# RMSNorm with GELU on one core: row squares and 1/rms moved to VectorE, one whole last store, gamma in two transfers

## The chip, the cores and the metric

The kernel runs on one core of a Trainium2 chip; the other cores run nothing. Profiles name the engines of a core so: PE is TensorE (PEld its weight loads), DVE is VectorE, ACT is ScalarE, POOL is GpSimd, SP is SyncE; 16 DMA engines move data between HBM and the core's memory. The metric is the device time of one execution in microseconds, as a median of several executions. A profiled execution gives a span, from its first to its last instruction, about 2 us under the time. Every execution told of here is at a granted clock of 1.0.

## The reference

```python
batch, seq_len, hidden = 8, 1024, 2048          # x: 64 MiB of float32
rms = np.sqrt(np.mean(x ** 2, axis=-1, keepdims=True) + eps)
out = gamma * x / rms
return 0.5 * out * (1 + np.tanh(np.sqrt(2 / np.pi) * (out + 0.044715 * out ** 3)))
```

The 8192 rows are independent. The output is as large as the input, so 67.1 MB come in and 67.1 MB go out.

## The kernel before

The rows are taken in 16 groups of 128 partitions x 4 rows x 2048 columns, 4 MiB each, which rotate through six buffers. A group is loaded from the queue of SP; ACT squares each row and sums it; POOL makes 1/rms of the sums; DVE multiplies by gamma (spread over the partitions once, in PSUM); ACT applies GELU with 1/rms as its scale and stores from its own queue. A buffer is loaded again when its store has landed.

```python
store_pieces = {
    0: [(R, [(0, NARROW), (NARROW, R * D)])],              # a narrow first piece
    G - 1: [(1, [(r * D, r * D + D)]) for r in range(R)],   # last group: a store for each row
}
scale_pieces = {G - 1: [(0, 1), (1, 1), (2, 1), (3, 1)]}

def squares(g):                                             # ACT
    for r in range(R):
        nc.scalar.activation(out=junk, in_=slot[g % SLOTS][:, r, :],
                             func=ACT.Square, accum_out=ssq[:, g, r : r + 1])

def inverse_rms(g):                                         # POOL, six small operations
    v = nc.gpsimd
    v.tensor_scalar(out=ms, in0=ssq[:, g, :], ...)          # mean + eps
    v.tensor_tensor(out=y, in0=ms, in1=power, op=ALU.pow)   # ** -0.5
    ...                                                     # one Newton step, four operations

# ... cut: scale (DVE), gelu_store (ACT)
for k in range(0, D, CHUNK):                                # CHUNK = 512: four transfers
    nc.scalar.dma_start(out=gamma_row[...], in_=gamma[k : k + CHUNK]...)
for g in range(SLOTS):
    load(g)
# ... cut
for g in range(G + 1):
    if g < G:
        squares(g); inverse_rms(g); scale(g)
    if g:
        gelu_store(g - 1)
        if g - 1 + SLOTS < G:
            load(g - 1 + SLOTS)
```

Of the kernel before, what the change touches and what calls it, by code (L numbers as in the profile page):

```python
# [1 line left out]

# [4 lines left out]

FP32 = mybir.dt.float32
ALU = mybir.AluOpType
ACT = mybir.ActivationFunctionType  # L10

P = 128
ROWS = 4
SLOTS = 6

GW = 32
CHUNK = 512

NARROW = 128


@with_exitstack
def kernel(
    ctx: ExitStack,
    tc: tile.TileContext,
    x: bass.AP,
    gamma: bass.AP,
    eps: bass.AP,
    out: bass.AP,
):  # L30




    nc = tc.nc
    D = x.shape[-1]
    R = ROWS
    eps_f = float(eps)
    x3 = x.rearrange("b s d -> (b s) d").rearrange("(g p r) d -> g p r d", p=P, r=R)
    o3 = out.rearrange("b s d -> (b s) d").rearrange("(g p r) d -> g p r d", p=P, r=R)  # L40
    G = x3.shape[0]

    sbuf = ctx.enter_context(tc.tile_pool(name="sbuf", bufs=1))
    psum = ctx.enter_context(
        tc.tile_pool(name="psum", bufs=1, space=bass.MemoryType.PSUM)
    )
    slot = [sbuf.tile([P, R, D], FP32, name=f"slot{i}") for i in range(SLOTS)]
    gamma_row = sbuf.tile([1, D // GW, GW + 4], FP32, name="gamma_row")
    ones = sbuf.tile([1, P], FP32, name="ones")
    warm = sbuf.tile([1, 1], FP32, name="warm")  # L50
    power = sbuf.tile([P, R], FP32, name="power")
    ssq = sbuf.tile([P, G, R], FP32, name="ssq")
    rstd = sbuf.tile([P, G, R], FP32, name="rstd")
    ms = sbuf.tile([P, R], FP32, name="ms")
    y = sbuf.tile([P, R], FP32, name="y")
    z = sbuf.tile([P, R], FP32, name="z")
    gamma_ps = psum.tile([P, D], FP32, name="gamma_ps")
    junk = psum.tile([P, D], FP32, name="junk")


    whole = [(R, [(0, R * D)])]
    store_pieces = {
        0: [(R, [(0, NARROW), (NARROW, R * D)])],
        G - 1: [(1, [(r * D, r * D + D)]) for r in range(R)],
    }
    scale_pieces = {G - 1: [(0, 1), (1, 1), (2, 1), (3, 1)]}

    def load(g):
        nc.sync.dma_start(out=slot[g % SLOTS], in_=x3[g])  # L69

    def squares(g):
        for r in range(R):
            nc.scalar.activation(  # L73
                out=junk,
                in_=slot[g % SLOTS][:, r, :],
                func=ACT.Square,
                accum_out=ssq[:, g, r : r + 1],
            )

    def scale(g):  # L80
        for r, n in scale_pieces.get(g, [(0, R)]):
            rows = slot[g % SLOTS][:, r : r + n, :]
            nc.vector.tensor_tensor(  # L83
                out=rows,
                in0=rows,
                in1=gamma_ps.unsqueeze(1).to_broadcast([P, n, D]),
                op=ALU.mult,
            )

    def inverse_rms(g):  # L90

        v = nc.gpsimd
        v.tensor_scalar(  # L93
            out=ms, in0=ssq[:, g, :], scalar1=1.0 / D, scalar2=eps_f,
            op0=ALU.mult, op1=ALU.add,
        )
        v.tensor_tensor(out=y, in0=ms, in1=power, op=ALU.pow)  # L97
        v.tensor_tensor(out=z, in0=y, in1=y, op=ALU.mult)  # L98
        v.tensor_tensor(out=z, in0=z, in1=ms, op=ALU.mult)  # L99
        v.tensor_scalar(  # L100
            out=z, in0=z, scalar1=-0.5, scalar2=1.5, op0=ALU.mult, op1=ALU.add
        )
        v.tensor_tensor(out=rstd[:, g, :], in0=z, in1=y, op=ALU.mult)  # L103

    def gelu_store(g):
        flat = slot[g % SLOTS].rearrange("p r d -> p (r d)")
        dst = o3[g].rearrange("p r d -> p (r d)")
        row = 0
        for n, stores in store_pieces.get(g, whole):
            for r in range(row, row + n):  # L110
                nc.scalar.activation(  # L111
                    out=slot[g % SLOTS][:, r, :],
                    in_=slot[g % SLOTS][:, r, :],
                    func=ACT.Gelu_apprx_tanh,
                    scale=rstd[:, g, r : r + 1],
                )
            row += n
            for a, b in stores:
                nc.scalar.dma_start(out=dst[:, a:b], in_=flat[:, a:b])  # L119

    with tc.manual_schedule():
        for k in range(0, D, CHUNK):
            nc.scalar.dma_start(
                out=gamma_row[:, k // GW : (k + CHUNK) // GW, 0:GW],
                in_=gamma[k : k + CHUNK].rearrange("(o a b) -> o a b", o=1, b=GW),
            )
        for g in range(SLOTS):
            load(g)
        nc.gpsimd.memset(power, -0.5)  # L129
        nc.vector.memset(warm, 0.0)  # L130
        nc.vector.memset(ones, 1.0)  # L131
        nc.scalar.activation(out=warm, in_=warm, func=ACT.Gelu_apprx_tanh)  # L132
        for k in range(0, D, CHUNK):
            nc.tensor.matmul(  # L134
                out=gamma_ps[:, k : k + CHUNK],
                lhsT=ones,
                rhs=gamma_row[:, k // GW : (k + CHUNK) // GW, 0:GW],
                start=True,
                stop=True,
            )  # L140
        for g in range(G + 1):
            if g < G:
                squares(g)
                inverse_rms(g)
                scale(g)
            if g:
                gelu_store(g - 1)
                if g - 1 + SLOTS < G:
                    load(g - 1 + SLOTS)


# [1 line left out]
_INS = ['x', 'gamma', 'eps']  # L153
_OUTS = [((8, 1024, 2048), 'float32')]

_NUMBERS = {'eps': 9.999999747378752e-06}


# [26 lines left out]
```

## Time and profile before

| | before |
|---|---|
| time, three runs | 317.45 us (317.38 to 317.48) |
| ACT / DVE / POOL busy | 251.2 / 139.4 / 32.3 us of 315.5 |
| DMA: 134.25 MB over the span | 426 GB/s |
| one square on ACT, with the read of its sum | 1.881 + 0.186 us |
| one multiplication by gamma, four rows | 8.69 us |

### The profile page before, as it was taken

What the parts mean: (1) busy time and instruction counts of PE and PEld (TensorE: products, weight loads), DVE (VectorE), ACT (ScalarE), POOL (GpSimd) and SP (SyncE); (2) the same over time, 40 slices, a digit from 0 to 9 for tenths busy, and PEclk for the clock granted to TensorE, in tenths of its full rate; (3) what the DMA queues carried; (4) which work ended last, traced back from release to release, by engine and by line L of the source; (5) the groups of instructions that cost most, each with busy time, mean ns of one, the idle gap of its engine ahead of it and who ended that gap; (6) DMA issues with size and microseconds to landing.
All of it is one profiled execution on the core that took longest, in us unless ns stands there. A gap on an engine that the chain in (4) does not pass through costs nothing.

```text
span 315.5 us, 479 instructions
## 1 busy us (share of the span) xinstructions
PE 7.9 (3%) x8; PEld 2.1 (1%) x8; DVE 139.4 (44%) x21; ACT 251.2 (80%) x194; POOL 32.3 (10%) x101
## 2 busy tenths in 40 slices
PE   0810000000000000000000000000000000000000
PEld 0200000000000000000000000000000000000000
DVE  0028909091918282827328082370824609480000
ACT  1289999999999999989596895969959599598500
POOL 0020202020202020202020020200202002020000
DMA  8999999999999999999999999999999999999997
GB/s 329 404 461 403 459 413 396 453 406 462 403 461 407 457 407 458 411 453 416 449 428 440 432 432 432 432 440 424 446 416 453 411 453 411 453 415 449 416 418 314
DMA packets 5315, 134.25 MB, mean 426 GB/s; under 512 B 704, under 2 KB 832, under 8 KB 832
## 3 DMA queue, kind: packets, MB, share of 16 engines
q1 hardware_dynamic: 2304, 67.11, 49.7%
q10 hardware_dynamic: 3008, 67.12, 49.4%
q14 instruction: 3, 0.02, 0.0%
HBM read 67.12 MB, written 67.11 MB: 425 GB/s over the span
## 4 chain that ended last, share of the span: by engine, by line
ACT 38%; DMA 32%; another core or an unknown queue 18%; issue 5%; ACTq 1%; SPq 0%
ACT slot L111 21%; DMA slot<-in_x_dram 16%; ACT junk L73 16%; DMA out_dram<-slot 15%; ACTq L119 1%; SPq L69 0%; ACTq L111 0%; ACTq L73 0%
## 5 line engine op out<-in xcount | busy, mean ns | idle before, releaser
L83 DVE TENSOR_TENSOR slot<-slot,gamma_ps 128x8192 f32<-128x8192 f32 (+1 forms) x19 | 139.2, 7338 | 142.3 <-ACT junk L73 142.3
L73 ACT ACTIVATE junk<-slot 128x2048 f32<-128x2048 f32 x64 | 120.4, 1881 | 40.8 <-DMA slot<-in_x_dram 36.8
L111 ACT ACTIVATE slot<-slot,rstd 128x2048 f32<-128x2048 f32 x64 | 123.0, 1987 | 1.7 <-ACT slot L111 1.7
L93 POOL TENSOR_SCALAR ms<-ssq 128x4 f32<-128x4 f32 x16 | 3.1, 194 | 242.8 <-ACT junk L73 242.8
L97 POOL TENSOR_TENSOR y<-ms,power 128x4 f32<-128x4 f32 x16 | 16.1, 1009 | 1.3
L73 ACT ACTIVATION_READ_ACCUMULATOR junk<-slot 128x1 f32 x64 | 11.9, 186 | 0.0
L134 PE MATMUL gamma_ps<-gamma_row,ones 1*128 1x512 f32 x8 | 7.9, 1112 | 9.2 <-DMA gamma_row<-in_gamma_dram 9.2
L132 ACT ACT_TABLE_LOAD x1 | 1.3, 1283 | 3.3 <-issue 3.3
L99 POOL TENSOR_TENSOR z<-z,ms 128x4 f32<-128x4 f32 x16 | 3.2, 201 | 1.3
L103 POOL TENSOR_TENSOR rstd<-z,y 128x4 f32<-128x4 f32 x16 | 3.2, 200 | 1.3
L98 POOL TENSOR_TENSOR z<-y 128x4 f32<-128x4 f32 x16 | 3.2, 200 | 1.3
L100 POOL TENSOR_SCALAR z<-z 128x4 f32<-128x4 f32 x16 | 3.1, 195 | 1.4
L134 PEld LDWEIGHTS gamma_ps<-gamma_row,ones 1*128 1x128 f32 x8 | 2.1, 306 | 13.4 <-issue 8.7
L130 DVE MEMSET warm<- 1x1 f32 x1 | 0.1, 59 | 0.8 <-PEq L166 0.8
L132 ACT ACTIVATE warm<-warm 1x1 f32<-1x1 f32 x1 | 0.2, 203 | 0.0
L131 DVE MEMSET ones<- 1x128 f32 x1 | 0.2, 165 | 0.0
L129 POOL MEMSET power<- 128x4 f32 x1 | 0.1, 102 | 0.3 <-POOLq L166 0.3
L166 POOL MEMSET const-float32-0.0<- 128x1 f32 x1 | 0.1, 99 | 0.2 <-issue 0.2
L166 POOL MEMSET const-bfloat16-1.0<- 128x1 bf16 x1 | 0.1, 102 | 0.0
L166 POOL MEMSET const-uint8-127<- 128x1 uint8 x1 | 0.1, 102 | 0.0
L166 POOL MEMSET const-float32-1.0<- 128x1 f32 x1 | 0.1, 99 | 0.0
## 6 DMA issues: line engine op xcount, KB each, us to landing
slot<-in_x_dram SPq DMA_DIRECT2D x16, 4096.0 KB, 29.9
out_dram<-slot ACTq DMA_DIRECT2D x14, 4096.0 KB, 43.3
out_dram<-slot ACTq DMA_DIRECT2D x4, 1024.0 KB, 17.5
out_dram<-slot ACTq DMA_DIRECT2D x1, 4032.0 KB, 28.5
gamma_row<-in_gamma_dram ACTq DMA_DIRECT2D x4, 2.0 KB, 10.3
out_dram<-slot ACTq DMA_DIRECT2D x1, 64.0 KB, 14.4
```

The lines of the kernel that those rows point to most:

```text
L73: nc.scalar.activation(out=junk, in_=slot[g % SLOTS][:, r, :], func=ACT.Square, accum_out=ssq[:, g, r : r + 1],)
L83: nc.vector.tensor_tensor(out=rows, in0=rows, in1=gamma_ps.unsqueeze(1).to_broadcast([P, n, D]), op=ALU.mult,)
L93: v.tensor_scalar(out=ms, in0=ssq[:, g, :], scalar1=1.0 / D, scalar2=eps_f, op0=ALU.mult, op1=ALU.add,)
L97: v.tensor_tensor(out=y, in0=ms, in1=power, op=ALU.pow)
L98: v.tensor_tensor(out=z, in0=y, in1=y, op=ALU.mult)
L99: v.tensor_tensor(out=z, in0=z, in1=ms, op=ALU.mult)
L100: v.tensor_scalar(out=z, in0=z, scalar1=-0.5, scalar2=1.5, op0=ALU.mult, op1=ALU.add)
L103: v.tensor_tensor(out=rstd[:, g, :], in0=z, in1=y, op=ALU.mult)
L111: nc.scalar.activation(out=slot[g % SLOTS][:, r, :], in_=slot[g % SLOTS][:, r, :], func=ACT.Gelu_apprx_tanh, scale=rstd[:, g, r : r + 1],)
L119: nc.scalar.dma_start(out=dst[:, a:b], in_=flat[:, a:b])
L132: nc.scalar.activation(out=warm, in_=warm, func=ACT.Gelu_apprx_tanh)
L134: nc.tensor.matmul(out=gamma_ps[:, k : k + CHUNK], lhsT=ones, rhs=gamma_row[:, k // GW : (k + CHUNK) // GW, 0:GW], start=True, stop=True,)
```

## The change

The intent is to relieve ACT, to shorten the small chain that makes 1/rms, and to have fewer transfers. In each group one or two of the four row squares go to DVE (22 of 64). All of 1/rms but the power goes to DVE, in four operations in place of five. The last group has one store in place of four. Gamma comes in two transfers in place of four; its row is now the first partition of the buffer that takes the throw-away squares of DVE.

```diff
-GW = 32
-CHUNK = 512
+GW = 64
+CHUNK = 1024
-    gamma_row = sbuf.tile([1, D // GW, GW + 4], FP32, name="gamma_row")
+    spare = sbuf.tile([P, D // GW, GW + 8], FP32, name="spare")
+    gamma_row = spare[0:1]
-        G - 1: [(1, [(r * D, r * D + D)]) for r in range(R)],
+    flat_pieces = {0: [(0, NARROW), (NARROW, R * D)]}
+    def on_vector(g):
+        return 1 if g % 3 else 2
+    def squares_on_vector(g, r, n):
+        for q in range(r, r + n):
+            row = slot[g % SLOTS][:, q, :].rearrange("p (a b) -> p a b", b=GW)
+            nc.vector.scalar_tensor_tensor(
+                out=spare[:, :, 0:GW], in0=row, scalar=1.0, in1=row,
+                op0=ALU.bypass, op1=ALU.mult, accum_out=ssq[:, g, q : q + 1])
-        v = nc.gpsimd
+        v = nc.vector        # ... the power alone stays on nc.gpsimd, then three operations
-                squares(g)
-                inverse_rms(g)
-                scale(g)
+                squares(g, 0, R - on_vector(g))
+                squares_on_vector(g, R - on_vector(g), on_vector(g))
+                # ... inverse_rms and scale; in the last group scale of row 0 comes first
```

## The prediction

> **What bounds the kernel now.** I read the engine shares first, then the transfer rates, then the waits, and only then the two ends of the span in order of time. From the page of the profiled run of the kernel before:
>
> ```profile
> span 315.5 us, 479 instructions
> ...
> PE 7.9 (3%) x8; PEld 2.1 (1%) x8; DVE 139.4 (44%) x21; ACT 251.2 (80%) x194; POOL 32.3 (10%) x101
> ...
> DMA  8999999999999999999999999999999999999997
> GB/s 329 404 461 403 459 413 396 453 406 462 403 461 407 457 407 458 411 453 416 449 428 440 432 432 432 432 440 424 446 416 453 411 453 411 453 415 449 416 418 314
> ...
> q1 hardware_dynamic: 2304, 67.11, 49.7%
> q10 hardware_dynamic: 3008, 67.12, 49.4%
> ```
>
> No compute engine is full: ACT has 80%, and it is what the change relieves. The DMA row has a 9 in every slice but the first and the last, and the two queues together took 49.7 + 49.4 = 99.1% of the 16 engines' span. 0.991 x 315.5 = 312.6 us of packet time on each engine, in a span of 315.5. So 2.9 us at most are not packet time, and those are the first microseconds before a packet moves and the last ones after it. The bytes are the same after the change: 16 loads and 16 stores of 4 MiB.
>
> The same over stretches (columns: stretch, length, busy time of PE, PEld, DVE, ACT, POOL, clock, DMA share, GB/s):
>
> ```profile
> 60.00:270.00 210.00, 0.00 (x0) 0.00 (x0) 104.25 (x12) 182.24 (x140) 23.98 (x72) 1.00 1.00 434
> 270.00:300.00 30.00, 0.00 (x0) 0.00 (x0) 8.88 (x4) 23.58 (x16) 2.00 (x6) 1.00 1.00 431
> 304.00:313.00 9.00, 0.00 (x0) 0.00 (x0) 0.00 (x0) 0.00 (x0) 0.00 (x0) 1.00 1.01 425
> 314.00:315.50 1.50, 0.00 (x0) 0.00 (x0) 0.00 (x0) 0.00 (x0) 0.00 (x0) 1.00 0.00 0
> ```
>
> DMA share is 1.00 from 60 to 313 us, with compute beside it or without. From 304 to 313 us no engine does anything, and the stores alone fill the DMA engines. The rate there is 425 GB/s, not 434: that is the last group, cut in four. The waits say who is early:
>
> ```profile
> POOL ms L93 <- ACT junk L73: 242.8, 16, 20.8
> DVE slot L83 <- ACT junk L73: 142.3, 16, 20.6
> ACT junk L73 <- DMA slot<-in_x_dram: 36.8, 10, 8.7
> ```
>
> DVE and POOL wait for ACT, and ACT waits for loads. A quicker ACT therefore only waits longer for loads. The chain of waits itself names ACT with 38%, but it is a chain through whichever wait came last, and the rows above show that for all of its length the DMA engines were full. I give the chain no weight.
>
> The tail, in order of time:
>
> ```profile
> 271.61 1.88 ACT L73 ACTIVATE junk<-slot 128x2048 f32<-128x2048 f32 x1 [3.68 <-DMA slot<-in_x_dram]
> ...
> 287.31 0.34 ACTq L119 DMA_DIRECT2D out_dram<-slot  x1
> ...
> 289.80 0.34 ACTq L119 DMA_DIRECT2D out_dram<-slot  x1
> ...
> 297.05 0.34 ACTq L119 DMA_DIRECT2D out_dram<-slot  x1
> ```
>
> The last load lands at about 271.5, and the last group's stores are issued from 289.80 to 297.05. But by the landing records of the trace the store of group 14 lands only at 304.5 and the four pieces of group 15 at 306.9, 309.4, 311.8 and 314.3. The last group stands in a queue for 10 us after it is ready.
>
> **What the Trainium skill says.** "DMA: Bandwidth & Descriptors", section "Where 436 GB/s comes from", gives 16 ports x 256 bits x 850 MHz = 435.2 GB/s as what the ports carry. The trace agrees: 434 GB/s over 210 us. The middle is at its ceiling and no change of engine work can help it. The same page, "Issuing engines are not separate DMA queues", says transfers started by different engines share the same 16 DMA engines and interleave. The trace agrees, with 49.7% and 49.4% for the load and store queues. "SBUF — State Buffer", section "SBUF: two separate sides", says compute ports and DMA ports do not contend. So 22 more rows read by DVE should not slow a packet; the trace shows a median 32 KiB packet of 1.213 us both beside busy engines and at the idle end. "VectorE: DVE Perf Modes", section on the TRN2 errata, gives a two-input fp32 op (N + 151)/0.96 ns, 2.29 us for 2048. The trace has 2.278 to 2.280 us for the 128x2048 multiplication.
>
> **The change, part by part.**
>
> *22 squares off ACT.* One costs 1.881 + 0.186 (accumulator read) = 2.07 us, so ACT loses 22 x 2.07 = 45.5 us and goes from 251 to about 206 us (65%). DVE gains 22 x about 2.35 = 52 us (an estimate: 2.28 for a two-input fp32 row, some 0.07 for writing the accumulator).
>
> *1/rms.* POOL loses five of six operations, 16 x 5 x 0.2 = 16 us, and keeps the power, 1.009 us each. DVE gains four small operations a group, 64 x about 0.15 us = 10 us, and stands still for the power and the two hand-overs, some 1.5 us a group. DVE comes to 139 + 52 + 10 = 201 us busy, 225 us with those waits.
>
> *Per group.* Loads land every 19.36 us in the middle (landing records). DVE needs 8.69 + 1.375 x 2.35 + 2.1 = 14.0 us a group, ACT 2.625 x 2.07 + 4 x 1.9 + 0.7 = 13.7 us. Both fit with 5 us to spare, so the queues stay filled. Worth to the end: 0.
>
> *Start.* The scratch rows of the new squares share their buffer with gamma, so the first of them waits for the last gamma matmul (at about 17 us now, against the first load's landing at 13.5). Then 2 x 2.35, about 2.5 for 1/rms and 8.7 for the multiplication put group 0's first activation near 33 us instead of 31. This is hidden: six loads of 9.7 us are queued from the first microsecond, so the queues hold work until 58 us whenever the first store comes. Worth: 0.
>
> *Tail.* Load 15 still lands near 271. ACT then has 2 squares (4.1), the activations of group 14 (7.7) and group 15 (8), so the one whole store is issued near 271.6 + 4.1 + 7.7 + 0.4 + 8 = 292 us. The queue runs empty only at 304.5, so there are 12 us to spare. DVE's side (4.7 + 2.3 + 2.5, then three rows of 2.3) ends at 288, before the last activation needs it. The wait for all four rows costs nothing. What does change is the packets. The four quarter stores land 2.453 us apart, 9.81 us for 4 MiB; the two whole stores before them land 9.68 us apart, also with nothing else in flight. Worth: 9.81 - 9.68 = 0.13 us. The packet records say the same: 0.309 us for 8 KiB, four of which make 1.236 against 1.213 for 32 KiB; times 8 packets an engine this is 0.18.
>
> *Gamma.* Each transfer puts 4 packets of 13 ns and one of 9 ns on every engine, 0.06 us. Two fewer save 0.12 us at most, and part overlaps the neighbours: the load that lands after the last of them came 9.70 us after the one before it, against 9.68 later. Worth: about 0.05.
>
> Sum: -0.13 - 0.05, about -0.2 us. 317.45 - 0.2 = 317.25 us, a gain of 0.06%.
>
> **The rivals.** (1) The relief of ACT shortens the run by several per cent, as its 80% and its 38% of the chain suggest; the tail alone would give 297 - 292 = 5 us, 312 us. Against it: DMA share 1.00 throughout and 10 us of queue behind the last store. The floor at 434 GB/s is 134.25 / 0.434 = 309.3 us of transfer, some 2.9 of ends and the 2 us by which the timed run exceeds the span: about 314. Nothing can give more than 1%. (2) The whole last store, kept until its fourth row is done, leaves the DMA engines idle. It would have to be issued after about 302 instead of 292; DVE would have to need over 10 us more in the last group. If a square on DVE took twice my 2.35 us the tail would still hold; the time would stay. (3) DVE becomes the bound: it would need over 19.4 us a group, 5 more than my sum. At 22 us a group the time would be about 350 us; nothing in the 2.28 us row suggests it. (4) Some packets are slow: 16 at the start take about 2 us, and 32 loads between 45 and 49 us, when the first stores begin, take 1.3 to 2.0 us in place of 1.21. Over 16 engines these two bursts cost some 0.7 us each. The changed kernel's first stores start at another moment and may meet a smaller or larger burst: between 0.6 us less and 0.4 us more. This is the largest thing I can't compute, larger than the gain.
>
> **Range and chances.** The middle is the sum, 317.25. The three runs before lie within 0.1 us. The burst gives 0.6 below and 0.4 above: 316.7 to 317.7. Two per cent is 6.3 us. Faster by that is under the floor; slower by that needs idle DMA engines, for which 5 us a group and 10 us at the tail stand as margins. I give each side 1%.
>
> **What will show it.** DMA share still 9 in all the slices but the ends, near 434 GB/s in the middle; ACT about 206 us, DVE about 200, POOL about 16; ACT's wait for loads grown from 37 us to some 80 (the 45 us returned as waiting); the last store issued near 292 and landing some 20 us later; 496 fewer DMA packets (4 x 144 - 144 for the store, 64 for gamma), and the 4 MiB of the last group in 9.68 us. The prediction is wrong if a slice in the middle falls under 9, if a load is issued late because a store was, or if the last store finds an empty queue.

## The result, and the profile after

| | before | after |
|---|---|---|
| median of four runs | 317.47 us | 317.32 us |
| lowest to highest | 317.38 to 318.16 | 317.24 to 317.67 |

The ratio is 0.9993, with a 95% interval of 0.9975 to 1.001: no change that the timing can resolve. Here and below a ratio is the mean time of one kernel's fast runs over that of the other's of the same rounds, so it is not quite the ratio of the medians quoted. A second series of six runs of the changed kernel (the run e11 below) gave 317.36 us.

The page of the changed kernel, the same rows as in the prediction's first fence:

```profile
span 315.3 us, 463 instructions
...
PE 7.2 (2%) x8; PEld 2.5 (1%) x8; DVE 198.6 (63%) x129; ACT 207.0 (66%) x150; POOL 16.4 (5%) x21
...
DMA  8999999999999999999999999999999999999996
GB/s 333 412 453 416 452 395 404 461 403 461 417 449 420 442 424 441 420 445 424 441 424 441 428 436 432 432 432 432 432 436 436 428 445 420 453 412 453 412 453 279
...
q1 hardware_dynamic: 2304, 67.11, 49.7%
q10 hardware_dynamic: 2512, 67.12, 49.3%
```

ACT lost 44 us, DVE gained 59, POOL lost 16, and the span moved by 0.2. The DMA row is as full as it was. Load packets are the same 2304; the store queue has 496 fewer.

The waits of the changed kernel (engine, line, releaser: us in total, times, longest):

```profile
POOL y L95 <- DVE ms L90: 263.1, 16, 19.7
ACT junk L72 <- DMA slot<-in_x_dram: 77.4, 12, 9.5
DVE spare L82 <- DMA slot<-in_x_dram: 29.1, 10, 4.1
...
DVE z L98 <- POOL y L95: 19.0, 16, 1.2
```

Here is where most of the 44 us went. ACT's wait for loads was 36.8 us and is 77.4: it waits 40.6 us longer for the same loads. DVE now waits for loads as well, which in the kernel before it never did. When two engines wait for the same transfers and the DMA engines never stand idle, the transfers are the bound.

What the moved work costs on DVE, from the groups of the changed kernel (count | busy us, mean ns of one | idle us before it, and what ended most of that):

```profile
L82 DVE SCALAR_TENSOR_TENSOR spare<-slot 128x2048 f32<-128x2048 f32 x22 | 50.4, 2290 | 43.6 <-DMA slot<-in_x_dram 29.1
...
L82 DVE DVE_READ_ACCUMULATOR spare<-slot 128x1 f32 x22 | 1.8, 82 | 0.0
```

And the tail in order of time (start us, length us, engine, line, operation; ACTq is the issue of a transfer):

```profile
271.94 1.88 ACT L72 ACTIVATE junk<-slot 128x2048 f32<-128x2048 f32 x1 [5.73 <-DMA slot<-in_x_dram]
...
283.58 0.34 ACTq L127 DMA_DIRECT2D out_dram<-slot  x1
...
291.73 0.34 ACTq L127 DMA_DIRECT2D out_dram<-slot  x1
```

The last store is issued at 291.73 us; in the kernel before the last piece was issued at 297.05. By the landing records the store ahead of it lands at 304.24 us, and this one at 313.92. It was ready 5 us earlier and stood 5 us longer in the queue. (A landing here is the end of the last of a transfer's 16 completion packets, one for each DMA engine. The semaphore update that engines wait for is recorded 0.3 to 0.8 us later.)

### The profile page after: what moved, and what is told of

Its sections match the earlier page's. It is cut to its first block, busy times and chain, and to the rows that moved or that the text cites. A ratio compares the mean times of both kernels' runs of the same rounds, so it can differ in the third digit from the quotient of the medians.

```text
span 315.3 us, 463 instructions
## 1 busy us (share of the span) xinstructions
PE 7.2 (2%) x8; PEld 2.5 (1%) x8; DVE 198.6 (63%) x129; ACT 207.0 (66%) x150; POOL 16.4 (5%) x21
## 3 DMA queue, kind: packets, MB, share of 16 engines
q1 hardware_dynamic: 2304, 67.11, 49.7%
## 4 chain that ended last, share of the span: by engine, by line
another core or an unknown queue 36%; DMA 27%; DVE 16%; ACT 7%; PE 2%; issue 2%; POOL 1%; SPq 1%; ACTq 0%; DVEq 0%; POOLq 0%
DMA out_dram<-slot 14%; DVE slot L109 11%; DMA slot<-in_x_dram 10%; ACT slot L120 7%; DVE spare L82 4%; DMA spare<-in_gamma_dram 2%; PE gamma_ps L142 2%; POOL y L95 1%; SPq L68 1%; ACT junk L72 1%; DVE ms L90 0%; DVE z L98 0%; DVE z L99 0%; DVE rstd L102 0%
## 5 line engine op out<-in xcount | busy, mean ns | idle before, releaser
L72 ACT ACTIVATE junk<-slot 128x2048 f32<-128x2048 f32 x42 | 79.0, 1882 | 79.8 <-DMA slot<-in_x_dram 77.4
L82 DVE SCALAR_TENSOR_TENSOR spare<-slot 128x2048 f32<-128x2048 f32 x22 | 50.4, 2290 | 43.6 <-DMA slot<-in_x_dram 29.1
L95 POOL TENSOR_TENSOR y<-ms,power 128x4 f32<-128x4 f32 x16 | 16.1, 1007 | 263.1 <-DVE ms L90 263.1
L90 DVE TENSOR_SCALAR ms<-ssq 128x4 f32<-128x4 f32 x16 | 2.7, 170 | 24.2 <-ACT junk L72 22.8
L98 DVE TENSOR_TENSOR z<-ms,y 128x4 f32<-128x4 f32 x16 | 2.6, 164 | 19.0 <-POOL y L95 19.0
L72 ACT ACTIVATION_READ_ACCUMULATOR junk<-slot 128x1 f32 x42 | 7.8, 186 | 0.0
L142 PE MATMUL gamma_ps<-spare,ones 1*128 1x512 f32 x8 | 7.2, 1073 | 8.1 <-DMA spare<-in_gamma_dram 8.1
L102 DVE SCALAR_TENSOR_TENSOR rstd<-z,y 128x4 f32<-128x4 f32 x16 | 2.6, 163 | 0.5
L99 DVE SCALAR_TENSOR_TENSOR z<-z,y 128x4 f32<-128x4 f32 x16 | 2.6, 163 | 0.5
L142 PEld LDWEIGHTS gamma_ps<-spare,ones 1*128 1x128 f32 x8 | 2.5, 325 | 11.2 <-issue 10.7
L82 DVE DVE_READ_ACCUMULATOR spare<-slot 128x1 f32 x22 | 1.8, 82 | 0.0
```

The lines of the kernel that those rows point to most:

```text
L72: nc.scalar.activation(out=junk, in_=slot[g % SLOTS][:, q, :], func=ACT.Square, accum_out=ssq[:, g, q : q + 1],)
L82: nc.vector.scalar_tensor_tensor(out=spare[:, :, 0:GW], in0=row, scalar=1.0, in1=row, op0=ALU.bypass, op1=ALU.mult, accum_out=ssq[:, g, q ...
L90: v.tensor_scalar(out=ms, in0=ssq[:, g, :], scalar1=1.0 / D, scalar2=eps_f, op0=ALU.mult, op1=ALU.add,)
L95: nc.gpsimd.tensor_tensor(out=y_, in0=m_, in1=power, op=ALU.pow)
L98: v.tensor_tensor(out=z_, in0=m_, in1=y_, op=ALU.mult)
L99: v.scalar_tensor_tensor(out=z_, in0=z_, scalar=-0.5, in1=y_, op0=ALU.mult, op1=ALU.mult)
```

## The experiments

Eleven runs were made, of ten new kernels and of the changed kernel once more; all gave the reference's result. "Before" is the kernel before in the same rounds on the same chip.

| run | what it is | median us (runs) | before | ratio, 95% interval |
|---|---|---|---|---|
| e1_store_only | before + whole last store | 317.65 (5) | 317.43 | 1.0006, 0.9993 to 1.0019 |
| e2_gamma_only | before + gamma in two | 317.53 (5) | 317.43 | 1.0003, 0.9991 to 1.0015 |
| e3_compute_only | the compute half alone | 317.31 (5) | 317.43 | 1.0001, 0.9989 to 1.0013 |
| e4_vector_3of4 | after, 48 squares on DVE | 317.90 (4) | 317.40 | 1.0012, 0.9997 to 1.0027 |
| e5_vector_4of4 | after, 64 squares on DVE | 350.18 (4) | 317.40 | 1.1032, 1.1014 to 1.105 |
| e6_before_extra2 | before + 2 squares a group on ACT | 351.49 (4) | 317.40 | 1.1069, 1.1053 to 1.1086 |
| e7_after_extra2 | after + the same 2 | 317.29 (4) | 317.40 | 0.9998, 0.9983 to 1.0013 |
| e8_no_narrow | after, group 0 in one store | 317.83 (6) | 317.43 | 1.0015, 0.9997 to 1.0033 |
| e9_tail_plus4 | after, last group 8.1 us later | 317.42 (6) | 317.50 | 0.9991, 0.9969 to 1.0013 |
| e10_tail_plus8 | after, last group 16.3 us later | 323.53 (6) | 317.50 | 1.0185, 1.0161 to 1.021 |
| e11_after_again | the changed kernel again | 317.36 (6) | 317.50 | 0.9993, 0.997 to 1.0016 |

The theory is that the DMA engines bind from the first microseconds to the last, so that compute is worth nothing until a margin is used up. The main rival is that ACT's relief, or the last group's work, is on the path, with its effect cancelled by something else that the change makes longer.

### The parts one by one

e1, the last store alone:

```diff
-        G - 1: [(1, [(r * D, r * D + D)]) for r in range(R)],
```

> The kernel before with one whole store for the last group and nothing else of the change. Theory (the DMA engines bound the run, only packet count and size move it): the last store, issued near 297.4 us, still waits behind the store of group 14; the two landings are 9.68 us apart in place of 9.81, so the last landing falls by 0.13 us; time 0.1 us under the kernel before, within noise. Rival (the wait for the fourth row empties the queues): a gap between the landings of the last two stores above 9.7 us and a longer time.

Measured: 317.65 us. The landing records give the part itself. The stores of groups 14 and 15 land 9.681 us apart. In each of the three profiles with four quarter stores (before, e2, e3) the distance is 9.81 us, and in each of the seven with a whole store that still queued (after, e1, e4, e7, e8, e9, e11) it is 9.68. So the 0.13 us are real, and they are the same in every profile. Yet the last landing did not fall: it came at 314.94 us, later than the 314.29 of the kernel before. One of the 16 DMA engines finished 1.2 us after the rest in this run. That spread between the engines varies from run to run by more than the whole gain.

e2, gamma alone:

```diff
-GW = 32
-CHUNK = 512
+GW = 64
+CHUNK = 1024
-        for k in range(0, D, CHUNK):      # matmuls
+        for k in range(0, D, 512):
```

> The kernel before with gamma in two transfers and nothing else. After the change, load 0 landed at 12.49 us in place of 12.81, which is more than the 0.05 us that I gave gamma. If fewer gamma packets did that, load 0 lands near 12.5 here too and the last landing falls by some 0.2 to 0.3 us; if it was chance in the first slow packets, load 0 lands near 12.8 and the last landing falls by 0.05. Time 317.1 to 317.4 either way.

Measured: 317.53 us. Load 0 landed at 12.73 us, nearer to the second forecast, but the last landing, 314.08 us, was 0.2 us under that of the kernel before, as in the first. One profile does not decide; all of them together do better. Load 0 landed at 12.81, 12.69, 12.66 and 12.65 us with four transfers (before, e1, e3, e6) and between 12.49 and 12.76 us with two (nine profiles, mean 12.64). The means differ by 0.06 us, with a spread of 0.27 within the second set. So the 0.3 us by which load 0 came earlier in the first profile of the change were mostly chance, and the last landing has the same scatter. The second profile of the changed kernel, e11, says the same: 12.70 us, where 12.5 to 12.75 had been forecast if 12.49 was chance (time 317.36 us, 317.2 to 317.5 expected). What repeats exactly is small: the first of the 16 completions of load 1 follows that of load 0 by 9.70 us with four transfers and by 9.68 with two. The semaphores show one thing more, which does not reach the end of the run: the update of load 0 that lets ACT start is recorded at 13.44 to 13.53 us in the four profiles with four transfers and at 12.94 to 13.20 us in the nine with two. Why it lags the packets more with four stays open.

e3, the compute half alone; against the changed kernel this puts back the transfers:

```diff
-GW = 64
-CHUNK = 1024
+GW = 32
+CHUNK = 512
+            if g == G - 1:      # in gelu_store, after each row; the store below is skipped
+                nc.scalar.dma_start(out=dst[:, r * D : r * D + D], in_=flat[:, r * D : r * D + D])
```

> Only the compute half of the change: 1/rms on VectorE but for the power, 22 squares on VectorE; gamma in four transfers and four quarter stores for the last group as before. Theory: no effect on the time, 317.4 to 317.5, the last landing within 0.2 us of the kernel before although ACT has 45 us less to do and waits 40 us longer for loads. Rival (relief of ACT shortens the run): the same few tenths of a microsecond as the whole change, or more.

Measured: 317.31 us, ratio 1.0001. ACT is busy 207.4 us there and waits 73.4 us for loads. All of the moved compute together is worth nothing in time, as the theory says. The rival as it was put, relief of ACT in net, is out. A gain from ACT cancelled by DVE's new work would look the same here; e7, which puts more than that work back on ACT alone, speaks against it.

### How much work the loads hide

e4 and e5, more squares on DVE:

```diff
-        return 1 if g % 3 else 2
+        return 3                  # e4; e5: return 4
```

> The changed kernel with three of four row squares on VectorE in every group. In the changed kernel's trace VectorE working without a gap needs 12.83 us a group with one square and each more is 2.33, so 17.5 us here, under the 19.36 us at which loads land. From 15.3 us on: 16 x 17.5 = 280, so group 15 is done near 295 and its store is issued near 298, before the queue runs dry at 304. Theory: 317.2 to 317.6, no change, with VectorE near 250 us. Rival (VectorE work beside transfers slows them, or the wait for the power counts): slower by over 1 us.

> All four squares on VectorE: 19.83 us a group, half a microsecond over the 19.36 us of the loads. Theory: the bound moves to VectorE. From 15.3 us on 16 x 19.83 = 317 us, so the last multiplication ends near 332, and with 2 us for the last activation, 9.7 for the store and 2 to the end the span is some 347 us, the time 349 (some +10%). Rival (a margin that the trace does not show): still near 317, or over 355.

From e4 the page's rows, then the issue of its last store:

```profile
PE 7.2 (2%) x8; PEld 2.5 (1%) x8; DVE 257.5 (81%) x181; ACT 156.7 (50%) x98; POOL 16.4 (5%) x21
...
DMA  8999999999999999999999999999999999999996
```

```profile
297.46 0.34 ACTq L127 DMA_DIRECT2D out_dram<-slot  x1
```

The order of the engines is turned round, DVE 81% and ACT 50%, and the DMA row is the same. The store was issued at 297.46 us (298 expected) and landed 9.68 us after the one before it. The time, 317.90 us, is 0.3 us above my range. Its interval still contains 1, and its last landing, 314.69 us, again has one DMA engine 0.9 us behind the rest. Whether this kernel makes that spread larger or met it by chance, four runs cannot tell.

e5 took 350.18 us, where 349 was expected. Its rows:

```profile
PE 7.2 (2%) x8; PEld 2.5 (1%) x8; DVE 294.2 (84%) x213; ACT 124.7 (36%) x66; POOL 16.4 (5%) x21
...
DMA  8999999999999999999999999999999455280957
```

Note what the shares do not say. DVE has 84% here, and it is the bound; in e4 it has 81%, and it is not. It shows not in DVE's share but in the DMA row: 9 down to slice 31, then 4, 5, 5, 2. Up to 270 us loads were still in the queue; after the last one only stores are left, and they come at DVE's pace.

The 19.36 us of the loads are not the limit, though the time came out near the forecast: half a microsecond over it in 16 groups would cost 8 us, and e5 cost 32.8. In e4 too DVE waited for no load: its waits name only the power on POOL and gamma at the start.

```profile
ACT slot L120 <- DVE slot L109: 111.3, 18, 8.2
DVE z L98 <- POOL y L95: 19.0, 16, 1.2
...
DVE spare L82 <- PE gamma_ps L142: 14.4, 1, 14.4
```

What kept e4 harmless was time left at the end. Its last store was issued at 297.46 us; 0.84 us passed in e10 from an issue into an empty queue to the first packet; and the store ahead of it landed from 303.4 us on. That leaves 5 us, 0.3 us a group, so the limit for these 16 groups is near 17.8 us (an estimate). e5 leads back to the same value: DVE ran from 15.46 to 334.18 us, 19.92 us a group; 32.8 us over 16 groups are 2.05; 19.92 - 2.05 = 17.9. From e6 below, 20.16 - 34.1 / 16 = 18.0. No run lies between 17.5 and 19.9 us.

e6 and e7, two squares a group more on ACT, whose sums go to a tile that nothing reads:

```diff
+    def extra(g):
+        for r in range(2):
+            nc.scalar.activation(out=junk, in_=slot[g % SLOTS][:, r, :],
+                                 func=ACT.Square, accum_out=waste[:, r : r + 1])
```

> The kernel before with two extra squares a group on ACT, whose sums go nowhere. ACT needs 16.09 us a group in the kernel before; two more squares of 2.035 make 20.16, over the 19.36 us of the loads. Theory: ACT becomes the bound: 13.5 + 16 x 20.16 = 336 us when the last activation ends, some 5 us more for the last quarter store, time near 343 (+8%). Rival (ACT has more slack than its steps say): 317.

> The changed kernel with the same two extra squares a group on ACT. ACT needs 13.4 + 4.07 = 17.5 us a group, under 19.36. Theory: no effect, 317.2 to 317.6: the 45 us taken from ACT are headroom, not time. Rival: a slower run, since the waits between ACT and VectorE are now longer chains.

From e6, the page's rows and the issue of group 14's store:

```profile
PE 7.9 (2%) x8; PEld 2.1 (1%) x8; DVE 139.4 (40%) x21; ACT 315.2 (90%) x258; POOL 32.1 (9%) x101
...
DMA  8999999999999999999999999999999819082498
```

```profile
327.64 0.34 ACTq L129 DMA_DIRECT2D out_dram<-slot  x1
```

e6 took 351.49 us. The step was right (the activations of one group begin at 299.79 us, those of the next at 319.95: 20.16 us a group), and so was the end of ACT's work, 337.4 us against 336. But I had let 5 us follow it, and 12 did: the time is 8 us over what I wrote. The store of group 14 is issued at 327.64 us, only 10 us before the last piece, and the two groups need 9.7 us each on the DMA engines: 327.6 + 1 + 9.7 + 9.8 = 348.1, and the last landing is at 348.4. The expectation counted the last piece alone and forgot the group in front of it. Here the last two stores are the tail. In e5 they were issued 14.35 us apart, more than the 9.7 us that one takes, and there the last one alone is.

From e7:

```profile
PE 7.2 (2%) x8; PEld 2.5 (1%) x8; DVE 199.0 (63%) x129; ACT 270.9 (86%) x214; POOL 16.4 (5%) x21
...
DMA  8999999999999999999999999999999999999996
```

The same extra work that cost the kernel before 34 us costs the changed kernel nothing, at an ACT share of 86%. This is what the change bought: headroom on ACT, 16.1 us a group down to 13.4, and no time.

### How long the last store stands in the queue

e9 and e10 delay the last group: extra squares on ACT, between its two true ones and the activations of group 14.

```diff
+                if g == G - 1:
+                    extra(g, 4)      # e10: 8; each 2.035 us
```

> The changed kernel with four extra squares on ACT in the last group alone, behind its two true ones: 4 x 2.035 = 8.1 us more between the last load and both of the last stores. In the changed kernel's trace the store of group 14 is issued at 283.6 us while the store of group 13 lands from 293.6 to 294.6, and the store of group 15 at 291.7 against 303.3 to 304.2. So the first of the two has some 9 us to spare (with 1 us from issue to the first packet). Theory: 8.1 us fit, time 317.2 to 317.7. Rival (the last group's work is on the path that sets the end): 325.

> The same with eight extra squares, 16.3 us: the store of group 14 is issued near 299.9, after the queue has run dry at 293.6 to 294.6. First packet near 300.9, then two whole stores of 9.68 and 1 us of spread: last landing near 321.2 in place of 313.9. Theory: time near 324.5, 7 us more, so 9 of the 16.3 us are hidden. Rivals: all of it hidden (317.3); none of it (333.5).

e9: 317.42 us. Its last store was issued at 299.99 us, 8.3 us later than in the changed kernel, and landed at 314.15 us.

e10: 323.53 us. Stretches of its span (the last two columns are DMA share and GB/s):

```profile
294.00:301.00 7.00, 0.00 (x0) 0.00 (x0) 6.86 (x5) 6.53 (x5) 0.00 (x0) 1.00 0.18 76
301.00:313.00 12.00, 0.00 (x0) 0.00 (x0) 0.00 (x0) 6.91 (x4) 0.00 (x0) 1.00 1.02 437
```

The store of group 14 was issued at 299.80 us, after the queue had run dry, and in the 7 us before 301 the DMA engines are 18% busy. That hole is what the run is longer by. The last landing is at 320.27 us against 313.92, so of 16.3 us some 10 are hidden; I expected 9. I had added 1 us of spread between the engines' ends. After the hole the 16 engines start in step, and their completions of the two stores lie within 0.17 us of each other.

### The burst when the first stores begin

e8:

```diff
-    flat_pieces = {0: [(0, NARROW), (NARROW, R * D)]}
+    flat_pieces = {}
```

> The changed kernel without the narrow first piece of group 0's store: one whole store there too. If the burst of slow load packets (some 1.3 to 2.0 us against 1.21, near 44 to 47 us) belongs to the first full-size store packets meeting loads, it stays, moved to some 40 us, and the time stays within 0.3 us. If it belongs to the narrow 512-byte packets, it goes and the time falls by some 0.6 us.

Measured: 317.83 us, with runs from 316.87 to 318.91, the widest of all the changed kernels. The burst is still there, at 40.0 to 42.2 us: 31 load packets of 1.35 to 2.05 us. So it belongs to the moment when the first stores meet loads, not to the narrow piece. In this profile something else differs: load 4 and store 0 land together (61.90 us both), later pairs do too, and between 70 and 83 us store packets take 1.22 to 1.39 us in place of 1.21. The time is not clear of noise either way. Why loads are slow at that moment stays open.

No run here is faster than the changed kernel by more than noise, and none was to be expected: the rate from 60 to 270 us was 433 or 434 GB/s in every profile in which DMA binds.

## Why the prediction was right

The predicted time was 317.25 us and the measured one 317.32, in the range of 316.7 to 317.7 and within 2% as forecast.

- **The bound.** Shown. The DMA rows before and after are alike to one digit, e3 puts the compute half at a ratio of 1.0001, and only the runs that open a hole in the DMA row (e5, e6, e10) are slower. None of the prediction's three signs of being wrong appeared: no slice in the middle under 9, no empty queue at the last store, and no load issued late (from the seventh on each was issued earlier than before, the last at 240.58 us and not 242.11). What in the path of a transfer sets 434 GB/s, the ports as the cited page has it or something behind them, no run here separates.
- **The engine sums.** ACT 206 predicted, 207.0 measured; DVE about 200, 198.6; POOL about 16, 16.4; ACT's wait for loads some 80, 77.4. A square on DVE was put at 2.35 us and takes 2.290 + 0.082. The 0.07 us for the accumulator and the 0.15 us for a small operation had no trace behind them; the traces give 0.082 and 0.16 to 0.17.
- **The margin a group.** 14.0 us was predicted for DVE; a whole step with one square takes 12.83 us in the trace, each more 2.33, so 13.7 on the mean. That there was room was right; how much, and where it ends, was not. The prediction put the limit at 19.4 us (rival 3) and 350 us of time at 22 us a group; e5 took 350.18 us at 19.9. The limit lies near 17.9 by the three estimates under e5, so some 4 us were to spare and not 5, and e4 at 17.5 us stood close under it. The loads land 19.36 us apart only in the middle; a run of 16 groups has two ends, which the prediction left out of this sum.
- **The start.** The time was mis-sized, and it did not matter. The first activation came at 30.57 us and not near 33. The last gamma matmul ended at 15.24 us, not 17, since with both transfers landed early all eight ran on without a wait.
- **The tail.** 292 us predicted for the last store, 291.73 measured. The slack was given as 12 us behind the last store. e10 shows about 10: it is the store of group 14, issued one group earlier, that reaches the empty queue first. The prediction looked only at the last one. (For a delay of the last store alone its 12 us stay untested: e10 delays both.)
- **The store's 0.13 us.** Exact in every profile by landing distance. One reading that it gave as support does not bear it: the prediction took 425 GB/s from 304 to 313 us as the mark of the cut store. In the changed kernel, with one whole store, that stretch reads

```profile
304.00:313.00 9.00, 0.00 (x0) 0.00 (x0) 0.00 (x0) 0.00 (x0) 0.00 (x0) 1.00 0.95 411
```

  which is lower still. Nine microseconds hold about seven packets an engine, and the view counts each packet whole where it starts, so the edges decide the figure. With each packet counted by its part inside the stretch, the packet records give 427.6 GB/s before and 433.4 after. So the cut store does leave a mark, but not one that this view can show. The distance between landings was the sound measure.
- **Gamma's 0.05 us.** Not refuted, not resolved: 0.06 us between means, in a scatter of 0.27. Its working was wrong. The prediction gave every engine four packets of 13 ns in each transfer; the trace has one (64 packets of 128 bytes in four transfers, over 16 engines), as its own count of 64 fewer packets implies. So before it is 4 x (13 + 9) = 88 ns an engine, after it 2 x (18 + 9) = 54: a saving of 0.03 us, not 0.12 at most.
- **The burst.** Named as the largest unknown, it hardly moved: slow packets cost 1.46 us an engine in the first profile of before and 1.40 after. What varied was the spread between the engines at the end. The first completion of the last store or piece falls between 312.94 and 313.38 us in all ten profiles in which DMA binds, the last between 313.92 and 314.94.

That the middle of the forecast was hit to 0.07 us is luck, since the four runs scatter from 317.24 to 317.67. That 0.2 us separate the two medians proves none of this: it lies inside the interval, and e1, with one of the two savings, reads 0.2 us the other way.

## What to carry to other kernels

Ask first whether the transfers ever wait for the engines; if the DMA row has no hole, relief of the busiest engine turns into a longer wait of that engine and the time does not move. Find the margin in us a group and not in busy shares: 81% cost nothing here and 84% cost a tenth of the time. Work that margin out with both ends of the run, not from the pace in the middle alone: here that pace was 19.36 us and the limit near 17.9. A tail is judged by the stores that still queue behind one another, so look at the last two, and measure a small effect by the distance between landings where the total is noisier than the effect.

## What the Trainium skill lacked or had wrong

- "DMA: Bandwidth & Descriptors", section "Measured (HBM→SBUF, 128 partitions, SWDGE, issued from GpSimd)", gives 341 GB/s, 78%, for a transfer of 1 MB. Stores of 1 MiB from the ACT queue that stand behind one another land 2.453 us apart here, 427 GB/s, against 433 for 4 MiB (9.681 us). The page lacks the case of a filled queue, in which three more transfers cost 0.13 us in all.
- No page has the size of the spread between the DMA engines (that two of them are usually slower is said, without a figure): completions of one 4 MiB store lie 0.15 to 0.17 us apart when the engines start in step (e5, e10), and those of the last store or piece 0.9 to 1.8 us apart at the end of a run that never paused. Here that is larger than the gain of the change.
- No page has the slow packets at the moment when the first stores meet loads: 24 to 31 load packets of some 1.3 to 2.2 us in place of 1.213 in each of the kernels in which DMA binds, 0.7 to 0.9 us on each engine.
- "VectorE: DVE Perf Modes", section on the TRN2 errata, has no row for a two-input operation with an accumulator, and no page has a time for the read of the sum: for 128x2048 fp32 it took 2.290 us and 0.082 us for the read of the sum.
